# The first phase's norm factors move from the input to the sums, and the start of the kernel is put in another order

## The chip, the cores and the metric

The kernel runs on one core of a Trainium2 chip. The metric is the device time of one execution in microseconds (us); the kernel before takes 1038.08 us as the median of three runs (1037.84 to 1038.27). The engines are named as in the profile: PE (TensorE, matrix products), ACT (ScalarE), DVE (VectorE), POOL (GpSimd), and SP (SyncE, which here only issues DMAs).

## The reference

The reference is a trunk of two layers on x, 256 tokens of 1024 numbers in float32. Layer 0 is a SwiGLU feed-forward network (FFN), a hybrid mixer (state-space heads and attention heads), and a second FFN; layer 1 has a recurrent block in the middle. That makes six sub-layers, each of the form

```python
def rms_norm(x, g):
    y = xf * lax.rsqrt(jnp.mean(xf * xf, axis=-1, keepdims=True) + NORM_EPS)
    return y * g
def swiglu(x, w_in, w_out):
    gate, up = jnp.split(x @ w_in, 2, axis=-1)
    return (jax.nn.silu(gate) * up) @ w_out
...
h = swiglu(rms_norm(x, g[0]), ffn_w_in[layer, 0], ffn_w_out[layer, 0])
x = x + 0.5 * rms_norm(h, g[1])
```

The width inside an FFN is 2816, that is 22 blocks of 128 for the gate and 22 for the up part. The change concerns the first sub-layer alone: the first norm, and the product of its result with `ffn_w_in`.

The norm multiplies row i of x by one factor r_i = 1/sqrt(mean square + eps) and column k by g_k. Since the factor belongs to a whole row, (r x g) W = r (x g W): the factor can be applied to the input or to the sums.

## The kernel before, in words

The tokens are two tiles of 128 (t = 0, 1), the model width is eight blocks of 128 (k). Every product is made in split precision: a number is stored as a rounded high part and the remainder, and a product is the sum of high*high, high*low and low*high. Each weight slab (128 x 1024, 512 KB) is loaded by a DMA into one of five `raw` buffers, ScalarE writes the high part (`act.copy`, L271), and VectorE the remainder (L272). The function `prepare(n)` does this for the first n slabs of the program's order, and `load` issues the DMAs. The normed and transposed input, high and low, is the tile `xT`.

The instructions of PE stand in the order in which the code issues them (`tc.manual_schedule`). A plan lists the steps of each phase; generators, such as `hidden_of`, wait for a number of microseconds of a clock that the code keeps for itself (`LAG`) and are taken up between the steps by `catch_up`. The other engines are ordered by the framework's scheduler; the helper `behind`, and `turn` in the first norm, fix an order on one engine where it is wanted. On each engine the instructions run in order, so one that waits holds those behind it.

The FFN's plan for phase 0 begins with six A steps, A(f, t) for f = 0, 1, 2 and t = 0, 1. An A step makes the gate and up sums of 128 tokens for block f (`a_tile`): for each k one product 512 wide (input high with both weight parts) and one 256 wide (input low with weight high), added up in one PSUM tile, gate and up side by side. `mm_wide` puts the first wide product first, then the narrow ones, then the other wide ones; with `groups` it does so for a part of the k at a time. A block needs two slabs, one for k = 0 to 3 and one for k = 4 to 7. `hidden_of` adds the two halves of the sum (`halves`: ScalarE copies, VectorE adds), applies Silu on ScalarE (L542), multiplies with the up part on VectorE (L543), and later has PE transpose the result (L146), which is split again (L315). After these come 19 B steps, B(f), for f = 3 to 21, with the weights as the stationary side: the sums come out transposed, 128 hidden channels by 256 tokens, gate and up in two PSUM tiles, so that no transpose is needed. O steps multiply the hidden tiles with the output weights; the hidden tile of B(f) is used two B steps later. At the end of the phase three O groups of six products stand between B(21) and the first use of its hidden tile.

The first norm (`first_norms`) begins at the start of the program. Five products of a tile of ones (`WARM`) are put on PE while the first DMAs run. The norm's weight g comes as one row and is spread over all partitions by two products with a matrix whose first row is one (`gain`, two PSUM tiles). For each token tile ScalarE squares the two halves of x and adds up along the row (L431), GpSimd makes the factor (L322, L323, a power of -0.5), and VectorE multiplies x by the gain (L437, `xg`) and the identity by the factor (L417, `dg`). A product of a 128 x 128 block of `xg` with `dg` then transposes and scales in one (16 products, PSUM tiles `side`), and ScalarE and VectorE split the result into `xT` (L315). The splits of the first and second slab are placed between.

In all later phases `pre_norm` scales x before it is transposed; the change doesn't touch it.

## Time and profile before

| what | us |
|---|---|
| median of three runs (lowest, highest) | 1038.08 (1037.84, 1038.27) |
| the profiled execution | 1037.15 |
| its span, first instruction to last | 1035.4 |
| PE busy in the span | 1022.0 |
| DVE, ACT, POOL busy | 718.3, 598.8, 24.6 |
| first product of x with the first slab, in the chain | 11.93 |

The span is what the traces show; the profiled execution's own time lies 1.75 us above it. In the trace a product of two float32 tiles appears as two records, one in the split precision as one, and matmul records overlap a little: the chain of waits gives their lengths without the overlap. `raw` is a slab as loaded, `w` a split slab, `rot` and `side` are PSUM tiles, `hid` a split hidden tile, `h` a hidden tile before its transpose, `half` the copy of half a sum, `r` a norm factor. An instruction's length and the distance to the next one differ, as neighbours on one engine overlap.

### The profile page before, as it was taken

How to read it: one execution, taken by the hardware profiler on the slowest of the kernel's cores; microseconds unless marked ns; L12 is line 12 of the kernel's file. 1: busy time of each engine (PE TensorE's matmuls, PEld its weight loads, DVE VectorE, ACT ScalarE, POOL GpSimd, SP SyncE). 2: the span in 40 equal slices, each digit the busy share in tenths (PEclk: the TensorE clock that was granted, in tenths of full speed). 3: DMA queues.
4: the chain of work that ended last, by engine and by line, in shares of the span. 5: the costliest groups of instructions: out<-in, count | busy, mean ns of one | idle time of the engine just before them, and what ended most of it. 6: DMA issues, size and time to landing. Idle time of an engine off the chain costs nothing.

```text
span 1035.4 us, 16026 instructions
## 1 busy us (share of the span) xinstructions
PE 1022.0 (99%) x6084; PEld 898.7 (87%) x6084; DVE 718.3 (69%) x1158; ACT 598.8 (58%) x1062; POOL 24.6 (2%) x60
## 2 busy tenths in 40 slices
PE   8999999999999999999999999999999999999997
PEld 7888888999989988888888888888899978888886
DVE  7865557589898777755657685655769878555663
ACT  7655546466566566555556574544659867455551
POOL 1000000100000001000000100000010010000000
PEclk9999999999999999999999999999999999999999
DMA  8966556275745473855557285656735367655521
GB/s 289 329 212 193 196 182 214 77 230 176 222 153 170 140 264 105 296 185 185 185 183 225 81 299 190 191 187 191 234 114 184 107 219 272 211 182 190 183 82 41
DMA packets 55746, 195.91 MB, mean 189 GB/s; under 512 B 6972, under 2 KB 8148, under 8 KB 55668
## 3 DMA queue, kind: packets, MB, share of 16 engines
q1 hardware_dynamic: 52464, 190.04, 56.3%
q10 hardware_dynamic: 3204, 4.84, 1.4%
q8 instruction: 48, 0.79, 0.3%
q14 instruction: 30, 0.25, 0.1%
HBM read 193.78 MB, written 1.07 MB: 188 GB/s over the span
## 4 chain that ended last, share of the span: by engine, by line
PE 89%; DVE 4%; ACT 3%; issue 2%; DMA 1%; POOL 1%; DVEq 0%; POOLq 0%; ACTq 0%
PE rot L142 57%; PE side L142 31%; PE rot L146 1%; DVE c L606 1%; ACT junk L334 1%; ACT w L271 1%; DVE w L272 1%; DMA ca<-rows 0%; DMA raw<-in_rec_out_dram 0%; POOL r L323 0%; DVE sc L957 0%; DVE xn L350 0%; DVE x L388 0%; POOL r L322 0%; DVE sc L955 0%
## 5 line engine op out<-in xcount | busy, mean ns | idle before, releaser
L142 PE MATMUL rot<-xT,w 128*128 128x256 f32 (+1 forms) x3512 | 562.1, 318 | 0.0
L272 DVE TENSOR_TENSOR w<-raw,w 128x1024 fp32r<-128x1024 f32 (+1 forms) x349 | 423.8, 1219 | 190.2 <-ACT w L271 189.3
L142 PEld LDWEIGHTS rot<-xT,w 128*128 128x128 f32 x3512 | 494.6, 187 | 51.9 <-issue 1.3
L271 ACT CAST w<-raw 128x1024 fp32r<-128x1024 f32 (+1 forms) x349 | 366.1, 1053 | 164.1 <-DMA raw<-in_ffn_out_dram 139.0
L142 PE MATMUL side<-w,hid 128*128 128x512 f32 x1056 | 253.6, 390 | 0.0
L142 PEld LDWEIGHTS side<-w,hid 128*128 128x128 f32 x1056 | 197.4, 188 | 41.3
L142 PE MATMUL rot<-w,xT 128*128 128x256 f32 (+1 forms) x768 | 117.1, 310 | 0.3 <-DVE sg L288 0.2
L142 PEld LDWEIGHTS rot<-w,xT 128*128 128x128 f32 x768 | 103.5, 188 | 9.3 <-DVE sg L288 1.0
L315 ACT CAST hid<-up 128x256 fp32r<-128x256 f32 x76 | 31.0, 407 | 98.2 <-DVE up L573 98.1
L287 ACT COPY half<-rot 128x256 f32<-128x256 f32 x176 | 63.7, 363 | 16.9 <-PE rot L142 16.9
L315 DVE TENSOR_TENSOR hid<-up,hid 128x256 fp32r<-128x256 f32 x76 | 32.3, 425 | 30.1 <-ACT hid L315 30.1
L288 DVE TENSOR_TENSOR sg<-rot,half 128x256 f32<-128x256 f32 x100 | 41.9, 419 | 13.5 <-ACT half L287 13.2
L142 PE MATMUL side<-w,os 128*128 128x512 f32 x192 | 45.5, 393 | 0.0
L571 ACT ACTIVATE sg<-sg 128x256 f32<-128x256 f32 x76 | 31.8, 419 | 23.6 <-DVE sg L288 23.6
L142 PEld LDWEIGHTS side<-w,os 128*128 128x128 f32 x192 | 35.6, 188 | 7.2
L288 DVE TENSOR_TENSOR up<-rot,half 128x256 f32<-128x256 f32 x76 | 31.9, 419 | 3.1 <-ACT half L287 3.1
L573 DVE TENSOR_TENSOR up<-sg,up 128x256 f32<-128x256 f32 x76 | 31.9, 420 | 0.2
L385 DVE TENSOR_TENSOR xn<-side,g_post 128x512 f32<-128x512 f32 x24 | 16.4, 690 | 20.0 <-ACT junk L334 19.6
L322 POOL TENSOR_SCALAR r<-ms 128x1 f32<-128x1 f32 x24 | 7.3, 302 | 857.8 <-ACT junk L334 852.6
L334 ACT ACTIVATE junk<-side 128x512 bf16<-128x512 f32 x24 | 14.4, 598 | 22.9 <-PE side L142 22.0
L350 DVE SCALAR_TENSOR_TENSOR xn<-x,r,g_pre 128x512 f32<-128x512 f32 x20 | 14.1, 749 | 17.3 <-POOL r L323 17.3
L142 PE MATMUL side<-w 128*128 128x512 f32 x96 | 22.8, 393 | 0.9 <-DVE w L315 0.7
(195 smaller groups left out, 505.5 us busy)
## 6 DMA issues: line engine op xcount, KB each, us to landing
raw<-in_ffn_in_dram SPq DMA_DIRECT2D x176, 512.0 KB, 4.5
raw<-in_ffn_out_dram SPq DMA_DIRECT2D x88, 512.0 KB, 4.6
raw<-in_hyb_cols_dram SPq DMA_DIRECT2D x36, 512.0 KB, 4.4
raw<-in_hyb_out_dram SPq DMA_DIRECT2D x16, 512.0 KB, 3.6
raw<-in_hyb_v_dram SPq DMA_DIRECT2D x8, 512.0 KB, 4.6
raw<-in_rec_a_dram SPq DMA_DIRECT2D x8, 512.0 KB, 5.1
raw<-in_rec_cols_dram SPq DMA_DIRECT2D x8, 512.0 KB, 4.1
raw<-in_rec_out_dram SPq DMA_DIRECT2D x8, 512.0 KB, 3.5
```

The lines of the kernel that those rows point to most:

```text
L142: pe.matmul(ps, lhsT=lhsT, rhs=rhs, start=start, stop=stop)
L146: pe.transpose(ps, src, ident)
L271: splits[:] = [behind(act.copy(w[0][:, c], raw[:, c]), hold)]
L272: splits.append(behind(dve.tensor_tensor(w[1][:, c], raw[:, c], w[0][:, c].bitcast(F32), op=ALU.subtract), hold))
L287: act.copy(tmp, ps[:, 256:512])
L288: dve.tensor_tensor(dst, ps[:, 0:256], tmp, op=ALU.add)
L315: return act.copy(hi, src), dve.tensor_tensor(lo, src, hi.bitcast(F32), op=ALU.subtract)
L334: behind(act.activation(junk, src, func=AF.Square, scale=1.0 / (32.0 * weight), accum_out=ms[:, h:h + 1]), firsts)
L350: dve.scalar_tensor_tensor(xn[h], xt[:, cols], r, state["g_pre"][:, cols], op0=ALU.mult, op1=ALU.mult)
L385: behind(dve.tensor_tensor(hg[h], acc[h], state["g_post"][:, cols], op=ALU.mult), firsts)
L571: act.activation(sg, sg, func=AF.Silu)
L573: dve.tensor_tensor(up, sg, up, op=ALU.mult)
```

## The change

The factors of the first phase no longer go to the input. Instead of the 16 products with `dg`, plain transposes of `xg` (x times the gain) are made (`flips`), and the sums are multiplied by the factor: in `hidden_of` the Silu takes `rs[t]` as its scale and VectorE multiplies by `rs[t]` as well; in the B steps, where tokens lie along the row, a tile `factors` is made once by two products of the factor with the identity and a copy, and VectorE multiplies the gate sum and GpSimd the up sum by it.

The order at the start changes too. The row of g is loaded by ScalarE's queue, and SyncE's queue now holds x0, slab 0, x1, slab 1 and so on (before: the row, x0, x1, slab 0, slab 1). VectorE scales x0 by the gain; ScalarE copies the gain out of PSUM into `gains`, and GpSimd scales x1 with the copy. The first two slabs are split in two pieces each, in turn with x0's halves. A second set of five warm-up products follows x0's transposes. The first A step takes its k in four groups of two, and the transposes of x1 stand between these groups (`second`, a generator). Of the four squares one stays ahead of the first splits; the other three come behind the splits of x1.

```diff
-    sp.dma_start(g_row[0:32, :], norm_g[0, 0:1, :].broadcast_to([32, DM]))
+    act.dma_start(g_row[0:32, :], norm_g[0, 0:1, :].broadcast_to([32, DM]))
     xs = [res.tile([P, DM], F32, name=f"x{t}") for t in range(NT)]
-    for t in range(NT):
+
+    def x_load(t):
         sp.dma_start(xs[t], x_in[t * P:(t + 1) * P, :])
 
+    x_load(0)
...
-    def prepare(n):
+    def prepare(n, pieces=1):
...
-            splits[:] = [behind(act.copy(w[0][:, c], raw[:, c]), hold)]
-            splits.append(behind(dve.tensor_tensor(w[1][:, c], raw[:, c], w[0][:, c].bitcast(F32), op=ALU.subtract), hold))
+            splits[:] = []
+            for p in range(pieces):
+                c = slice(p * width // pieces, (p + 1) * width // pieces)
+                splits.append(behind(act.copy(w[0][:, c], raw[:, c]), hold))
+                splits.append(behind(dve.tensor_tensor(w[1][:, c], raw[:, c], w[0][:, c].bitcast(F32), op=ALU.subtract), hold))
             split[key] = w
             load(ready[0] + RAW)
...
+        def square(t, h):
+            junk = work.tile([P, 512], BF16, name="junk", bufs=1)
+            turn(act.activation(junk, xs[t][:, h * 512:(h + 1) * 512], func=AF.Square, scale=1.0 / 32.0,
+                                accum_out=ms[t][:, h:h + 1]))
+            if h:
+                turn(*rstd_of(rs[t], ms[t], 1.0))
+
+        def scaled(engine, t, h, g):
+            turn(engine.tensor_tensor(xg[t][:, h, :], xs[t][:, h * 512:(h + 1) * 512], g, op=ALU.mult))
+
+        def flips(t, h):
+            ps = side()
+            for k in range(4):
+                flip(ps[:, k * P:(k + 1) * P], xg[t][:, h, k * P:(k + 1) * P])
+            dst = [xT[:, 4 * h:4 * h + 4, j, t * P:(t + 1) * P] for j in range(2)]
+            return dst[0], dst[1], ps.rearrange("p (k c) -> p k c", k=4)
+
+        def weights(n, pieces=1):
+            hold[:] = latest.values()
+            prepare(n, pieces)
+            turn(*splits)
+
+        def second():
+            for h in range(2):
+                yield 0.9
+                held = flips(1, h)
+                turn(*split_to(*held))
+            square(0, 1)
+            weights(3)
+            square(1, 0)
+            square(1, 1)
+            hold[:] = latest.values()
+            normed.add((0, 1))
+            norms.discard((0, 1))
 
         warm = rot()
-        for _ in range(WARM):
-            mm(warm[:, 0:P], ones, ones, True, True)
-        gain, xg, dg, rs = [], [], [], []
-
-        def scale(t):
-            turn(dve.tensor_scalar(dg[t], ident, rs[t], None, op0=ALU.mult))
-
+
+        def busy(n):
+            for _ in range(n):
+                mm(warm[:, 0:P], ones, ones, True, True)
+
+        load(1)
+        x_load(1)
+        load(RAW)
+        busy(WARM)
+        gain = []
+        ms = [work.tile([P, 2], F32, name="ms", bufs=4) for _ in range(NT)]
+        rs.extend(work.tile([P, 1], F32, name="r", bufs=4) for _ in range(NT))
+        slot = wp.tile([P, 2 * SLAB + LINES], F32, name="w", bufs=SPLIT)
+        xg = [slot[:, t * DM:(t + 1) * DM].rearrange("p (h c) -> p h c", h=2) for t in range(NT)]
         for h in range(2):
             gain.append(rot())
             mm(gain[h], first, g_row[:, h * 512:(h + 1) * 512], True, True)
-        for t in range(NT):
-            ms = work.tile([P, 2], F32, name="ms", bufs=4)
-            r = work.tile([P, 1], F32, name="r", bufs=4)
-            rs.append(r)
-            xg.append(begin.tile([P, 2, 512], F32, name="xg", bufs=2))
-            dg.append(begin.tile([P, P], F32, name="dg", bufs=2))
-            for h in range(2):
-                src = xs[t][:, h * 512:(h + 1) * 512]
-                junk = work.tile([P, 512], BF16, name="junk", bufs=1)
-                turn(act.activation(junk, src, func=AF.Square, scale=1.0 / 32.0, accum_out=ms[:, h:h + 1]))
-                if h:
-                    for ins in rstd_of(r, ms, 1.0):
-                        turn(ins)
-                    if not t:
-                        scale(t)
-                turn(dve.tensor_tensor(xg[t][:, h, :], src, gain[h], op=ALU.mult))
-        scale(1)
+        square(0, 0)
+        gains = begin.tile([P, NT, 512], F32, name="gains")
+        for h in range(2):
+            scaled(dve, 0, h, gain[h])
+            turn(act.copy(gains[:, h, :], gain[h]))
+        held = [flips(0, h) for h in range(2)]
+        busy(WARM)
+        for h in range(2):
+            scaled(pool, 1, h, gains[:, h, :])
+
         hold[:] = latest.values()
-        prepare(1)
-        for ins in splits:
-            turn(ins)
-        for t in range(NT):
-            for h in range(2):
-                ps = side()
-                for k in range(4):
-                    c = slice(k * P, (k + 1) * P)
-                    mm(ps[:, c], xg[t][:, h, c], dg[t], True, True)
-                dst = [xT[:, 4 * h:4 * h + 4, j, t * P:(t + 1) * P] for j in range(2)]
-                for ins in split_to(dst[0], dst[1], ps.rearrange("p (k c) -> p k c", k=4)):
-                    turn(ins)
-                if h and not t:
-                    hold[:] = latest.values()
-                    prepare(2)
-                    for ins in splits:
-                        turn(ins)
-            normed.add((0, t))
-        hold[:] = latest.values()
+        prepare(1, 2)
+        one = list(splits)
+        turn(*one[0:2])
+        turn(*split_to(*held[0]))
+        turn(*one[2:4])
+        turn(*split_to(*held[1]))
+        weights(2, 2)
+        normed.add((0, 0))
+        norms.add((0, 1))
         start_pool.__exit__(None, None, None)
-
+        spawn(second())
+
+    rs = []
     xT = new_xT(0)
     first_norms(xT)
...
+        def factors():
+
+            if not laid:
+                laid.append(hid.tile([P, NT * P], F32, name="factors"))
+                ps = rot()
+                for t in range(NT):
+                    mm(ps[:, t * P:(t + 1) * P], rs[t].broadcast_to([P, P]), ident, True, True)
+                act.copy(laid[0], ps[:, 0:256])
+            return laid[0]
...
-                act.activation(h32[:, 0:P], sg[:, 0:P], func=AF.Silu)
-                dve.tensor_tensor(h32[:, P:256], h32[:, 0:P], sg[:, P:256], op=ALU.mult)
+                if ph:
+                    act.activation(h32[:, 0:P], sg[:, 0:P], func=AF.Silu)
+                    dve.tensor_tensor(h32[:, P:256], h32[:, 0:P], sg[:, P:256], op=ALU.mult)
+                else:
+                    act.activation(h32[:, 0:P], sg[:, 0:P], func=AF.Silu, scale=rs[t])
+                    dve.scalar_tensor_tensor(h32[:, P:256], sg[:, P:256], rs[t], h32[:, 0:P], op0=ALU.mult, op1=ALU.mult)
...
                 until(lambda: (ph, t) in normed)
-                ps = a_tile(xT, t, s, (KT,) if ph or f else (KT // 2, KT // 2))
+                ps = a_tile(xT, t, s, (KT,) if ph or f or t else (2, 2, 2, 2))
                 until(lambda: len(turning) < 2)
...
                 halves(sg, pg)
+                if not ph:
+                    dve.tensor_tensor(sg, sg, factors(), op=ALU.mult)
                 act.activation(sg, sg, func=AF.Silu)
                 halves(up, pu)
+                if not ph:
+                    pool.tensor_tensor(up, up, factors(), op=ALU.mult)
                 dve.tensor_tensor(up, sg, up, op=ALU.mult)
...
         def gains():
             if not ph:
-                yield 10.0
+                yield 12.0
             state["g_post"] = g_tile(l, j + 1, "g_post")
```

On PE the start of the stream moves. `rot<-ones` are warm-up products, `rot<-g_row,first` the gains, `side<-dg,xg` the products that transpose and scale, `side<-ident,w` the plain transposes (the tile `xg` now lies in a slab buffer `w`), and `rot<-w,xT` the A steps. Before:

```order
L142 MATMUL rot<-ones 128x128 x5
L142 MATMUL rot<-g_row,first 128x512 x2
L142 MATMUL side<-dg,xg 128x128 x16
L142 MATMUL rot<-w,xT 128x512
L142 MATMUL rot<-w,xT 128x256 x4
L142 MATMUL rot<-w,xT 128x512 x3
L142 MATMUL rot<-w,xT 128x256 x4
```

Now, from the transposes of x0 on:

```order
L146 MATMUL side<-ident,w 128x128 x8
L142 MATMUL rot<-ones 128x128 x5
L142 MATMUL rot<-w,xT 128x512
L142 MATMUL rot<-w,xT 128x256 x2
L142 MATMUL rot<-w,xT 128x512
L142 MATMUL rot<-w,xT 128x256 x2
L142 MATMUL rot<-w,xT 128x512 x2
L146 MATMUL side<-ident,w 128x128 x4
L142 MATMUL rot<-w,xT 128x256 x2
L142 MATMUL rot<-w,xT 128x512 x2
L146 MATMUL side<-ident,w 128x128 x4
L142 MATMUL rot<-w,xT 128x256 x2
```

The 16 products in front of the first A step are gone; eight transposes and five warm-up products stand there, and two sets of four transposes stand inside the first A step.

On ScalarE the rows from the second slab on to the fourth and fifth: `raw` gives the slab (before: `raw_145` is slab 1, `raw_147` slab 2, `raw_149` slab 3; now `raw_107`, `raw_109`, `raw_111`), `half<-rot` are the copies of A(0,0)'s and A(0,1)'s sums. Before:

```order
L271 CAST w_169<-raw_145 128x1024
L315 CAST xT_103<-side_174 128x4x128
L315 CAST xT_103<-side_181 128x4x128
L271 CAST w_192<-raw_147 128x1024
L271 CAST w_197<-raw_149 128x1024
L271 CAST w_202<-raw_151 128x1024
```

Now:

```order
L276 CAST w_164<-raw_107 128x512 x2
L320 CAST xT_102<-side_184 128x4x128
L320 CAST xT_102<-side_195 128x4x128
L418 ACTIVATE junk_202,ms_120<-x0_83 128x512
L292 COPY half_222<-rot_175 128x256
L276 CAST w_206<-raw_109 128x1024
L588 ACTIVATE h32_225<-sg_221,r_122 128x128
L418 ACTIVATE junk_211,ms_121<-x1_84 128x512
L418 ACTIVATE junk_213,ms_121<-x1_84 128x512
L292 COPY half_271<-rot_253 128x256
L276 CAST w_228<-raw_111 128x1024
L588 ACTIVATE h32_274<-sg_270,r_123 128x128
```

Slabs 2 and 3 followed directly on the second tokens' `xT`; now a square, a copy of a sum and, ahead of slab 3, a Silu, two more squares and the copy of A(0,1)'s sums stand before them.

On PE behind B(3) (`rot<-xT,w` is a B step, `side<-w,hid` an O step), before:

```order
L142 MATMUL rot<-xT,w 128x512 x2
L142 MATMUL rot<-xT,w 128x256 x16
L142 MATMUL rot<-xT,w 128x512 x14
L142 MATMUL side<-w,hid 128x512 x6
L146 MATMUL rot<-ident,h_379 128x128
L142 MATMUL side<-w,hid 128x512 x12
L146 MATMUL rot<-ident,h_407 128x128
```

Now:

```order
L142 MATMUL rot<-xT,w 128x512 x2
L142 MATMUL rot<-xT,w 128x256 x16
L142 MATMUL rot<-xT,w 128x512 x14
L142 MATMUL rot<-ident,r 128x128 x2
L146 MATMUL rot<-ident,h_386 128x128
L142 MATMUL side<-w,hid 128x512 x12
L146 MATMUL rot<-ident,h_414 128x128
L142 MATMUL side<-w,hid 128x512 x12
```

The two products `rot<-ident,r` are added, and the transposes of two hidden tiles move by one O group. From there on the rows of all engines are the same but for the added multiplications in the B steps of phase 0: 19 rows on VectorE, L618, one in each B step, and 19 on GpSimd, L622.

## Rows read from the trace of the kernel before

**Rows 1.** The page's first part: engine, busy us, share, instructions.
```profile
PE 1022.0 (99%) x6084; PEld 898.7 (87%) x6084; DVE 718.3 (69%) x1158; ACT 598.8 (58%) x1062; POOL 24.6 (2%) x60
```

**Rows 2.** Chain of waits over the start: start us, us, what.
```profile
7.88 4.04 PE side L142 x32
11.93 8.37 PE rot L142 x48
20.30 0.11 PE rot L146
...
29.15 5.53 PE rot L142 x32
```

**Rows 3.** Timeline of TensorE, first 13 us: start, length, instructions.
```profile
1.10 2.50 PE L142 MATMUL rot<-ones 128*128 128x128 f32 x10 [1.10 <-DVE ones L188]
3.48 2.38 PE L142 MATMUL rot<-g_row,first 128*128 128x512 f32 x4
```

**Rows 4.** Timeline of VectorE at the start, shapes kept apart.
```profile
5.05 0.69 DVE L437 TENSOR_TENSOR xg<-x,rot 128x512 f32<-128x512 f32 x1 [2.44 <-PE rot L142]
...
13.20 1.28 DVE L315 TENSOR_TENSOR xT<-side,xT 128x512 fp32r<-128x512 f32 x2
14.40 2.35 DVE L272 TENSOR_TENSOR w<-raw,w 128x1024 fp32r<-128x1024 f32 x2
```

**Rows 5.** Timeline of the SyncE queue at the start.
```profile
1.24 0.89 SPq L185 DMA_DIRECT2D x<-in_x_dram  x2
2.16 13.81 SPq L252 DMA_DIRECT2D raw<-in_ffn_in_dram  x8
```

**Rows 6.** DMAs issued at 1.24 and 2.16: KB, us to landing.
```profile
x<-in_x_dram SPq DMA_DIRECT2D x1, 512.0 KB, 3.7
...
raw<-in_ffn_in_dram SPq DMA_DIRECT2D x1, 512.0 KB, 5.8
```

**Rows 7.** Timeline of ScalarE at the start, shapes kept apart.
```profile
4.98 0.63 ACT L431 ACTIVATE junk<-x 128x512 bf16<-128x512 f32 x1 [2.70 <-DMA x<-in_x_dram]
...
5.73 0.63 ACT L431 ACTIVATE junk<-x 128x512 bf16<-128x512 f32 x1
6.27 0.19 ACT L431 ACTIVATION_READ_ACCUMULATOR junk<-x 128x1 f32 x1
...
11.40 1.15 ACT L315 CAST xT<-side 128x512 fp32r<-128x512 f32 x2
12.45 2.95 ACT L271 CAST w<-raw 128x1024 fp32r<-128x1024 f32 x3
15.30 0.37 ACT L287 COPY half<-rot 128x256 f32<-128x256 f32 x1
15.56 1.06 ACT L271 CAST w<-raw 128x1024 fp32r<-128x1024 f32 x1
...
18.64 0.30 ACT L542 ACTIVATE h<-sg 128x128 f32<-128x128 f32 x1
```

**Rows 8.** The page's costliest groups: the post-norm's VectorE line.
```profile
L385 DVE TENSOR_TENSOR xn<-side,g_post 128x512 f32<-128x512 f32 x24 | 16.4, 690 | 20.0 <-ACT junk L334 19.6
```

**Rows 9.** Windows of TensorE: us, busy (count), granted clock, DMA.
```profile
7.88:11.93 4.05, 4.05 (x33) 1.00 1.00 406
```

**Rows 10.** Timeline of GpSimd at the start.
```profile
2.07 0.29 POOL masks.py:199 TENSOR_SCALAR_AFFINE_SELECT ident<-ident 128x128 f32<-128x128 f32 x1
...
6.94 0.57 POOL L323 TENSOR_TENSOR r<-r,power 128x1 f32<-128x1 f32 x1
```

**Rows 11.** Timeline of VectorE, last B tile of phase 0.
```profile
179.60 0.42 DVE L288 TENSOR_TENSOR sg<-rot,half 128x256 f32<-128x256 f32 x1 [1.47 <-ACT half L287]
...
183.40 0.43 DVE L315 TENSOR_TENSOR hid<-up,hid 128x256 fp32r<-128x256 f32 x1 [0.47 <-ACT hid L315]
```

**Rows 12.** Chain of waits at the end of phase 0.
```profile
180.69 12.24 PE side L142 x54
```

**Rows 13.** GpSimd's groups by line: busy, mean ns, idle before.
```profile
L323 POOL TENSOR_TENSOR r<-r,power 128x1 f32<-128x1 f32 x24 | 13.5, 563 | 2.0
```

14 lines of the change are left out of this document (7 added, 7 removed).

## The prediction

> **What bounds the kernel now.** I read the page's first part, then the chain of waits over the start, then each engine's timeline there. TensorE is busy for 99% of the span [rows 1], so a change gains only where it lets TensorE's stream of weight products begin earlier, or takes instructions out of it. In the chain that stream begins at 11.93 us: 48 products of three tiles A(f, t) run 8.37 us without a gap, and further tiles follow after single transposes [rows 2]. One A tile is 16 products, eight 512 wide and eight 256 wide, and takes 2.79 us (8.37 / 3): 0.233 for a wide one, 0.116 for a narrow one. So A(0,0) ends at 14.72, A(0,1) at 17.51, A(1,0) at 20.30. In front of the stream stand 16 products of the row-scaled input, 4.04 us from 7.88, and these waited for the norm factor. That is what the change attacks. I compare the moment when A(1,0) ends, because everything after it hangs on TensorE alone.
>
> **The start, worked out anew.** All times are from the span's start; a spacing is the distance between the starts of two neighbours.
>
> Until 5.86 nothing can move: five warm-up products end at 3.60, the two gain products at 5.86 [rows 3], and VectorE's first scaling starts at 5.05 when the first gain is there [rows 4]. x and the first slab arrive in time: x0 was issued at 1.24 and took 3.7 us (4.94), slab 0 as third came at 2.16 + 5.8 = 7.96 [rows 5, 6]; that is 1.5 us per transfer, so in the new order slab 0 comes by 6.5, x1 by 8.0, slab 1 by 9.5. The norm row moves to another queue; 128 KB in front of x become 128 KB beside x, which I cost at nothing, as it is needed at 3.48 only. If it came 0.5 us late, all below would come 0.5 later.
>
> VectorE scales x0's halves 5.05 to 5.74 and 5.88 to 6.57 (0.69 each [rows 4]). ScalarE squares the first half (0.75 spacing [rows 7]) and copies both gains out of PSUM; two engines that read one PSUM tile do so in turn here, as VectorE's post-norm does behind ScalarE's square of the same sums [rows 8]. So the copies start at 5.77 and 6.60. If they need not wait, the second starts 0.35 earlier. From 7.13 ScalarE rounds slab half, x half, slab half, x half, with 0.5 us for a slab half (half of 0.98, from three casts in 2.95) and 0.525 for an x half (two in 1.05) [rows 7]: the starts are 7.13, 7.65, 8.15, 8.7, then slab 1's halves from 9.5.
>
> VectorE follows with the remainders, 0.6 us each (two x halves in 1.28, a whole slab 1.14 [rows 4]), and is the slower: starts 7.75, 8.3, 8.9, 9.5, 10.1, 10.7. TensorE makes its first four transposes at 5.9 and the next at 6.6 (0.11 each [rows 2]), and then five warm products, 1.25 us at the rate of the 16 products (0.25 each): it is free at 8.4. [...] The first A product goes at 8.45, the narrow ones at 9.0, when the first x remainder is there. From 9.0 I find no wait: the rest of the tile is 2.79 - 0.23 = 2.56 and the eight transposes of the second tokens inside it are 0.88. A(0,0) ends at about 12.5 and A(0,1) at 15.3, each 2.2 us earlier than now.
>
> **What takes most of it back.** ScalarE's queue now holds more work ahead of the third and fourth slabs. The last x half of the second tokens can be rounded when its transposes are done, 0.70 us (the last group) before A(0,0) ends, at 11.85. Behind it stand, in ScalarE's order: the square of x0's second half, the copy of A(0,0)'s sums, slab 2, the Silu of A(0,0), two squares of x1, the copy of A(0,1)'s sums, and only then slab 3. With the spacings 0.53, 0.75, 0.26, 0.95, 0.2 (a Silu takes 0.30, and neighbours overlap by about 0.1), 0.75, 0.75 and 0.26 [rows 7] slab 3 starts at 16.3 and is rounded at 17.35; nothing in this row of work waits (the Silu needs the norm factor, done 13.1 + 1.05 = 14.15, from the end of the read of the accumulator at 6.46 to the end of the power at 7.51 [rows 7, 10]; the copy of A(0,1) needs 15.3). VectorE adds 1.22: slab 3's remainder is there at 18.6. In the kernel now these two slabs are split before 16.75 [rows 4], with TensorE needing them at 17.5. In the changed kernel TensorE comes to A(1,0) at 15.3, waits 0.4 for slab 2's remainder, about 1.0 for slab 3's rounding, and again some 0.1 for its remainder; its last four wide products, 0.93, end at 19.55. So at the end of A(1,0) the gain is 20.30 - 19.55 = 0.75 us.
>
> **The rest of the phase.** The tiles that follow find their slabs split (slabs 4 and 5 at 20 and 21.2, needed at 22.5), so the 0.75 is carried on. Two products of the factors against the identity come into the stream behind B3's products [rows 2]: 2 x 0.25 = 0.5 us, with nothing beside them. The first phase's 19 B tiles get one more VectorE multiplication each (0.42, the length of the sum's addition) and one of GpSimd. VectorE idles 1.47 us in front of such an addition at the end of the phase [rows 11] and a hidden tile is used two B tiles later, so this is hidden. The narrowest place is the last B tile: its remainder is done at 183.83 [rows 11], and TensorE needs the hidden tile first at 180.69 + 3 x 1.36 = 184.77 (54 products in 12.24 [rows 12]). VectorE's multiplication stands before a slab split that waits for ScalarE, so it costs nothing; GpSimd's stands in the chain. For 256 columns of two operands the trace has no row. The nearest: 0.29 us for 128 columns of one operand, of which some 0.1 is fixed, and 0.56 for one column of a power [rows 10, 13]. That makes 0.5 for one operand, and 0.9 for two read in turn; bounds 0.3 (VectorE does it in 0.42) and 1.5. I take 0.9: the chain ends at 184.7, TensorE does not wait. At 1.5 it would lose 0.4 us.
>
> **GpSimd in the start.** By the same rows a multiplication of 512 columns is 0.9 for one operand and 1.7 for two; bounds 0.5 and 3. From 8.0 two of them end at 11.4 with 1.7 each, when TensorE comes for the second at 11.35. I take 1.5. [...]
>
> **Sum.** -0.75 + 0.5 = -0.25 us. The profiled execution took 1037.15 us (span 1035.4 and 1.75 around it), which makes 1036.9; the median of the runs shown is 0.93 higher, so 1037.8.
>
> **The rivals.**
> 1. *The gain is kept.* If slab 3 isn't late (ScalarE gets through its row faster, or the squares are cheaper beside others), the 2.2 us stay: -2.2 + 0.5 = -1.7, 1036.4. For it: A(0,0) itself is bounded by few steps. Against it: the eight ScalarE instructions are in one order, and each has a row.
> 2. *GpSimd holds TensorE inside A(0,0).* TensorE takes its instructions in order, so the second tokens' transposes stop the stream until GpSimd is done. With p us for one multiplication the loss over my sum is 8.0 + 2p - 11.35; it begins at p = 1.7, the kernel is slower than before from p = 1.8, and by over 2 us from p = 2.85. At p = 2.5: +1.4, 1039.5. For it: no row of this size, and VectorE busy beside it. Against it: one operand of 128 columns takes 0.29.
> 3. *GpSimd's first multiplication is slow to begin.* Before, the first of the 24 powers took 0.57 us, as their mean of 0.563 [rows 10, 13], with no gap in front beyond the usual; a first use costs nothing there. [...] Worked out from the rows: if the first multiplication began d us late, the two would end at 11 + d, and the kernel would lose d - 0.6 against before (11 + d - 11.35 - 0.25); it is slower by over 2.1 us from d = 2.7, and d = 4 gives 1041.5.
> 4. *The clock falls before the second warm-up.* The first five products took 2.50 us, twice the later rate [rows 3]; then TensorE would be free at 9.65 and the narrow products would go at 9.9 and not at 9.0: 0.9 - 0.25 = +0.65, 1038.7. Against it: the clock granted after the idle time [rows 9].
>
> **Chances.** My forecast 0.58, rival 1 0.17, rival 2 0.13, rival 3 0.03, rival 4 0.05, something unseen 0.04. A measurement of this kernel tells about 0.2%, 2.1 us, from no change; only rival 1 with a little more, or something unseen, reaches faster (0.09), and rivals 2 and 3 at their upper ends reach slower (0.10). The likeliest case alone spans 1037.0 to 1038.8 (ScalarE's steps 0.3 either way, the norm row 0.5 late, the last B tile 0.4). The range reaches to rival 1 below and to rival 2 with p = 2.6 above: 1036.2 to 1039.8.
>
> **What would show it.** Right: the first A product near 8.5; A(0,1)'s sums near 15.3; then TensorE waiting for slab 3 for 1 us or more; A(1,0)'s end near 19.6; 0.5 us of `rot<-ident,r` behind B3; GpSimd's wide multiplications under 1.7 us. Wrong: a wait of the transposes for GpSimd; A(1,0) without a wait; a wait at the last B tile of the phase; any new wait behind 200 us.

## The result and the profile after

The changed kernel takes 1043.57 us (median of five runs, 1042.51 to 1044.55); the kernel before took 1037.92 beside it (1037.19 to 1038.27). The ratio is 1.0053, with a 95% interval of 1.0042 to 1.0065: slower by 5.65 us, where the forecast was 1037.8 and at most 1039.8. The profiled execution took 1043.57 with a span of 1041.8, 6.4 us over the span of before.

The page of the changed kernel: its first part, and the chain that ended last by engine; the last line is that chain in the kernel before. TensorE's share in the chain is the first thing to see: 63% where it was 89%, with VectorE, DMA and ScalarE in it for the rest. Busy time alone [rows 1] says almost nothing of the change.

```profile
PE 1025.3 (98%) x6082; PEld 898.9 (86%) x6082; DVE 732.2 (70%) x1175; ACT 600.8 (58%) x1067; POOL 44.1 (4%) x81
...
PE 63%; DVE 12%; DMA 11%; ACT 7%; issue 4%; POOL 1%; DVEq 0%; POOLq 0%; ACTq 0%; SPq 0%
```

```profile
PE 89%; DVE 4%; ACT 3%; issue 2%; DMA 1%; POOL 1%; DVEq 0%; POOLq 0%; ACTq 0%
```

**The start.** TensorE's timeline (start, length, instructions, idle time in front and what ended it). The gain products, which began at 3.48 [rows 3], begin at 5.10, after 1.49 us of waiting for the norm row; and they take 3.75 us, not 2.38. The first A product comes at 12.25, and the tile A(1,0) waits 0.64 us for a slab's rounding. The last line is the pair of factor products.

```profile
5.10 3.75 PE L142 MATMUL rot<-g_row,first 128*128 128x512 f32 x4 [1.49 <-DMA g_row<-in_norm_g_dram]
...
10.12 1.28 PE L142 MATMUL rot<-ones 128*128 128x128 f32 x10
12.25 1.94 PE L142 MATMUL rot<-w,xT 128*128 128x512 f32 x8 [0.85 <-ACT xT L320]
...
21.15 2.46 PE L142 MATMUL rot<-w,xT 128*128 128x256 f32 x11 [0.64 <-ACT w L276]
23.45 0.28 PE L146 MATMUL rot<-ident,h 128*128 128x128 f32 x1
...
37.83 0.60 PE L142 MATMUL rot<-ident,r 128*128 128x128 f32 x4
```

As a mark for the whole start I use the transpose that comes right behind A(1,0). In the timeline of before it stands at 20.14 (20.30 in the chain, without the overlap [rows 2]):

```profile
20.14 0.27 PE L146 MATMUL rot<-ident,h 128*128 128x128 f32 x1
```

So TensorE is 3.3 us late at this point. ScalarE's timeline of the changed kernel, with what stands in front of the fourth slab (the cast at 20.05): both copies of the gain wait for VectorE, and three squares lie ahead of that slab.

```profile
7.91 0.59 ACT L473 COPY gains<-rot 128x512 f32<-128x512 f32 x1 [1.66 <-DVE w L424]
9.61 0.59 ACT L473 COPY gains<-rot 128x512 f32<-128x512 f32 x1 [1.12 <-DVE w L424]
...
16.29 0.63 ACT L418 ACTIVATE junk<-x 128x512 bf16<-128x512 f32 x1
...
18.42 0.62 ACT L418 ACTIVATE junk<-x 128x512 bf16<-128x512 f32 x1
...
19.17 0.63 ACT L418 ACTIVATE junk<-x 128x512 bf16<-128x512 f32 x1
...
20.05 1.05 ACT L276 CAST w<-raw 128x1024 fp32r<-128x1024 f32 x1
```

**The end of phase 0.** Here the chain of before was TensorE alone [rows 12]. In the changed kernel the same stretch of the chain runs through VectorE, ScalarE and GpSimd, and the last B step's hidden tile comes 0.71 us too late for TensorE, at 189.24 (the chain, then TensorE's timeline):

```profile
184.94 0.96 ACT w L276
...
185.92 1.23 DVE w L277
...
187.56 0.74 POOL up L622
188.33 0.43 DVE up L623
188.78 0.41 ACT hid L320
...
189.24 2.79 PE side L142 x11
```

```profile
189.24 3.02 PE L142 MATMUL side<-w,hid 128*128 128x512 f32 x12 [0.71 <-ACT hid L320]
```

**Behind it** there is one more wait of the kind, in a later phase none of whose instructions were changed; before has none there.

```profile
737.43 4.83 PE L142 MATMUL rot<-xT,w 128*128 128x512 f32 x27 [0.78 <-DVE sg L293]
```

I laid TensorE's products of the two traces side by side, counted from the last. The lateness of the changed kernel is 3.31 us behind A(1,0), 3.77 behind the factor products, 4.64 behind the last B step of phase 0, 5.7 behind 737 us and 5.80 at the end. The remaining 0.6 of the 6.4 us of span is behind TensorE's last product (last section).

### The profile page after: what moved, and what is told of

It reads as the page before. It is cut to its first block, busy times and chain, and to the rows that moved or that the text cites. A ratio compares the mean times of both kernels' runs of the same rounds, so it can differ in the third digit from the quotient of the medians.

```text
span 1041.8 us, 16075 instructions
## 1 busy us (share of the span) xinstructions
PE 1025.3 (98%) x6082; PEld 898.9 (86%) x6082; DVE 732.2 (70%) x1175; ACT 600.8 (58%) x1067; POOL 44.1 (4%) x81
## 4 chain that ended last, share of the span: by engine, by line
PE 63%; DVE 12%; DMA 11%; ACT 7%; issue 4%; POOL 1%; DVEq 0%; POOLq 0%; ACTq 0%; SPq 0%
PE rot L142 40%; PE side L142 22%; DMA raw<-in_ffn_out_dram 11%; DVE w L277 6%; ACT w L276 4%; DVE sg L293 1%; ACT junk L339 1%; PE rot L146 1%; DVE c L656 1%; DVE xn L355 0%; DMA raw<-in_rec_out_dram 0%; POOL r L328 0%; DVE up L293 0%; DVE x L393 0%; DVE sc L1007 0%
## 5 line engine op out<-in xcount | busy, mean ns | idle before, releaser
L277 DVE TENSOR_TENSOR w<-raw,w 128x1024 fp32r<-128x1024 f32 (+1 forms) x351 | 431.2, 1234 | 182.0 <-ACT w L276 180.7
```

Of the source, the lines that this page charges most:

```text
L277: splits.append(behind(dve.tensor_tensor(w[1][:, c], raw[:, c], w[0][:, c].bitcast(F32), op=ALU.subtract), hold))
```

## The experiments

Each kernel ran beside the kernel before on the same chip. The third column is the difference of the two medians, and the ratio is to the kernel before. The chips differ: the medians of before lie between 1036.94 and 1037.92, so where two of the runs below are compared, the difference of their third columns stands in brackets. The marks are of one execution each; in ten traces with the change's own start (the change and runs 4, 6, 7, 9, 10 and 13 to 16) they lie between 22.90 and 23.56.

| run | us | above before | ratio (95%) | mark behind A(1,0) |
|---|---|---|---|---|
| the change | 1043.57 | 5.65 | 1.0053 (1.0042, 1.0065) | 23.45 |
| 1 norm row on SyncE's queue | 1041.58 | 4.02 | 1.0039 (1.0025, 1.0053) | 21.43 |
| 2 eight warm-up products | 1043.26 | 5.70 | 1.0057 (1.0045, 1.0070) | 22.61 |
| 3 before, row on ScalarE's queue | 1038.60 | 1.04 | 1.0007 (0.9998, 1.0016) | 21.28 |
| 4 no factors in the B steps | 1040.66 | 3.10 | 1.0030 (1.0018, 1.0041) | 22.90 |
| 5 fourth slab ahead of the squares | 1042.49 | 5.51 | 1.0057 (1.0042, 1.0073) | 22.42 |
| 6 up multiplied on VectorE | 1043.07 | 6.09 | 1.0058 (1.0045, 1.0070) | 23.35 |
| 7 no multiplication of up | 1043.33 | 6.35 | 1.0052 (1.0040, 1.0065) | 23.56 |
| 8 start alone (1, 4 and 5) | 1037.79 | 0.81 | 1.0005 (0.9997, 1.0014) | 20.29 |
| 9 no multiplication of the gate | 1041.39 | 4.18 | 1.0039 (1.0025, 1.0053) | 23.08 |
| 10 factor products only | 1041.36 | 4.15 | 1.0038 (1.0026, 1.0051) | 23.02 |
| 11 x1 scaled by VectorE | 1043.33 | 6.12 | 1.0060 (1.0046, 1.0074) | 22.32 |
| 12 mended, complete | 1039.32 | 2.11 | 1.0020 (1.0011, 1.0028) | 20.26 |
| 13 gate multiplied in the first ten B steps | 1043.40 | 6.46 | 1.0061 (1.0048, 1.0074) | 23.31 |
| 14 gate multiplied in the last nine | 1042.18 | 5.24 | 1.0052 (1.0038, 1.0066) | 23.50 |
| 15 the change, one more execution | 1044.31 | 7.37 | one time | 23.34 |
| 16 as 7, one more execution | 1041.49 | 4.55 | one time | 23.11 |

### 1. The norm row back on SyncE's queue

```diff
-    act.dma_start(g_row[0:32, :], norm_g[0, 0:1, :].broadcast_to([32, DM]))
+    sp.dma_start(g_row[0:32, :], norm_g[0, 0:1, :].broadcast_to([32, DM]))
```

> One line of the change undone: the row of g is loaded by SyncE's queue again, ahead of x0; all else as in the changed kernel. Theory (the row comes late on ScalarE's queue): TensorE does not wait for the row, the second gain is done near 5.9 us and not at 8.85, the first A product goes near 9.3 and not at 12.25, A(1,0) ends near 20.6 and not at 23.6, and the time falls by 3 us, to 1040.5. Rival (ScalarE's row of squares and GpSimd beside VectorE make most of the loss): the time falls by under 1 us, to 1042.6 or more, although the gains come early.

TensorE's timeline in that run: the gain products no longer wait, but still take a microsecond more than before.

```profile
3.55 3.38 PE L142 MATMUL rot<-g_row,first 128*128 128x512 f32 x4
```

The mark moves from 23.45 to 21.43 and the median falls by 2.0 us (1.6), where I had expected 3. The queue is the largest single part of the start's loss. The wait is not the only reason for slow gain products: here there is none, and they still take 3.38 us.

### 2. Eight warm-up products in front of the gain products

```diff
-        busy(WARM)
+        busy(WARM + 3)
         gain = []
```

> The changed kernel with eight warm-up products ahead of the gains in place of five, so that TensorE is not idle until the row lands at 5.1 us. Theory (the gain products are slow because TensorE was idle before them): the two gain products take about 2.0 us after 5.1 and not 3.75, and the time falls by 1.5 to 2 us, to 1041.7. Rival (they are slow whatever stands before them; only the landing counts): the pair still takes 3.7 us, and the time stays within 0.3 us of 1043.6.

The wait for the row is filled (the products end at 4.89), and the gain products take 2.53 us, near the 2.38 of before. The mark improves by 0.84 to 22.61, and the time stays: this profiled execution (1045.71, the slowest of its five) shows, at 167 us, a wait of 2.5 us for VectorE's `sg` that the change's first trace does not have. So an earlier mark need not show in the time: what TensorE gains at the start can be lost at the end of the phase.

### 3. The kernel before with the row on ScalarE's queue

The one line of the change, put into before.

> The kernel before, with the row of g loaded by ScalarE's queue, and nothing else changed. Theory: the row lands at about 5.1 us here too, the second gain is done near 8.9, and VectorE's scalings of x, which stand ahead of the first slab's remainder, end 1.1 us later; the time rises by 1.0 to 1.3 us, to 1039.1. Rival (the row is late only because x0 and slab 0 go in turn with it in the new order): the row lands by 3.5 us and the time stays at 1038.

```profile
4.80 3.75 PE L142 MATMUL rot<-g_row,first 128*128 128x512 f32 x4 [1.19 <-DMA g_row<-in_norm_g_dram]
```

Wait and slow gain products appear in before as well, and the mark is 1.14 us later; the median rises by 1.04 us, which the interval of the ratio does not tell from nothing. So the queue's price at the start doesn't need the rest of the change; in the changed kernel the mark loses more by it (2.0), which I put down to the new start hanging on the gain products as a whole, without a run that tests this.

### 4. No factors in the B steps

Left out: both multiplications of the 19 B steps, the factor products and their copy.

```diff
-                if not ph:
-                    dve.tensor_tensor(sg, sg, factors(), op=ALU.mult)
...
-                if not ph:
-                    pool.tensor_tensor(up, up, factors(), op=ALU.mult)
```

> The changed kernel without the factors on the gate and up sums of the 19 B steps (the two products, the copy, and the 19 multiplications each of VectorE and GpSimd are left out, so the B steps' sums are not scaled). Theory (the products cost 0.45 us in the stream, and GpSimd's multiplication in the last B step makes TensorE wait 0.9 us): the time falls by 1.3 us, to 1042.3, and A(1,0) ends at 23.6 as before. Rival (GpSimd beside VectorE's remainders delays slabs in the whole phase and what follows it): the time falls by 2.5 us or more.

2.9 us less than the change (2.6): the rival. There is no wait at the end of the phase, and the lateness of TensorE stays at 2.8 us from the mark to the end. So about half of the loss lies in the B steps, where I had put 0.5.

### 5. The fourth slab split ahead of the squares

```diff
-            weights(3)
+            weights(4)
             square(1, 0)
```

> The changed kernel with slab 3 split ahead of the two squares of x1 on ScalarE. Theory (the prediction's: ScalarE's row holds A(1,0)): TensorE's wait of 0.6 us for slab 3's rounding in A(1,0) goes, A(1,0) ends 0.6 to 1.0 us earlier against A(0,1)'s end, and the time falls by as much, to 1042.8. Rival (the wait moves to slab 2's remainder or to the Silu of A(0,1), or the gain is lost again later in the phase): the time stays within 0.3 us of 1043.6.

```profile
15.50 7.09 PE L142 MATMUL rot<-w,xT 128*128 128x256 f32 x36
22.42 0.27 PE L146 MATMUL rot<-ident,h 128*128 128x128 f32 x1
```

The wait for the slab is gone (36 products in one piece, where the change has 25 and then 11 behind a wait), and the mark is 1.0 us earlier. In the median this doesn't show: the executions lie between 1039.88 and 1044.71. The other kernels derived from the change that multiply the gate in B steps scatter by 1.4 to 3.9 us; those that don't multiply it (runs 4, 9, 10) by 0.7 to 1.0. This is a hint and no more, as five times are few: run 8 doesn't multiply it either, and its eleven times scatter by 2.2. The profiled execution, the fastest of the four, has no wait at the end of phase 0 although it does all the multiplications.

### 6. The multiplication of up on VectorE

```diff
-                    pool.tensor_tensor(up, up, factors(), op=ALU.mult)
+                    dve.tensor_tensor(up, up, factors(), op=ALU.mult)
```

> The changed kernel with the up sums of the B steps multiplied by the factors on VectorE in place of GpSimd. Theory (GpSimd's multiplication runs beside VectorE's slab remainder and stretches it from 1.23 to 1.7 us, which delays the slabs step by step until TensorE waits near the phase's end): no remainder of the phase is longer than 1.25 us, the last slabs come 1.5 to 3 us earlier, TensorE does not wait at the last B step, and the time falls by 1.5 to 2.5 us, to 1041.5, although VectorE does 19 multiplications more. Rival (VectorE's added work is what delays the slabs): the time rises, to 1044 or more.

No gain, and TensorE still waits, 0.85 us, at the last B step; so GpSimd's place in the chain isn't the cause. Two lines say why the two are about equal: the groups of VectorE's slab remainders by form, in the change and then here.

```profile
L277 DVE TENSOR_TENSOR w<-raw,w 128x1024 fp32r<-128x1024 f32 x346 | 427.5, 1241 | 180.8 <-ACT w L276 179.6
```

```profile
L277 DVE TENSOR_TENSOR w<-raw,w 128x1024 fp32r<-128x1024 f32 x346 | 420.6, 1220 | 181.1 <-ACT w L276 180.0
L622 DVE TENSOR_TENSOR up<-up,factors 128x256 f32<-128x256 f32 x19 | 8.0, 419 | 0.1
```

Given to GpSimd, the 19 multiplications lengthen VectorE's remainders by 6.9 us in all (run 7, without them, has 420.2); done by VectorE they take 8.0. The offload saves VectorE hardly anything.

### 7. No multiplication of up

Left out: GpSimd's multiplication in the B steps; VectorE's stays.

> The changed kernel without GpSimd's multiplication of the up sums (they are left unscaled); the factor products and VectorE's multiplications stay. Theory: as with the multiplication on VectorE, the remainders take 1.23 us; the time falls by 2.0 to 2.5 us, to 1041.3, and the run without any factors (1040.7) is better only by the two products, 0.45 us, and little more. Rival (the delay comes from VectorE's multiplication of the gate sums, which stands in front of the slab remainders): it falls by under 0.8 us.

No gain in the median, where I had expected 2.0 to 2.5 us, but here it is a poor guide: the five times are 1041.73, 1041.74, 1043.33, 1043.35 and 1043.48. In the profiled one TensorE doesn't wait at the end of phase 0, and waits 1.06 us for VectorE's `sg` at 1000.79, in a phase with no changed instruction (run 16 takes this up).

### 8. The new start alone

Runs 1, 4 and 5 together: the B steps' factors are left out, the row is on SyncE's queue, the fourth slab comes first.

> The changed kernel with three things at once: the row of g on SyncE's queue, slab 3 split ahead of the squares of x1, and no factors on the B steps' sums (these stay unscaled). It shows what the new order of the start gives by itself. Theory (the three losses add up: 2.0 + 0.7 + 2.9): 1038.0, no better than the kernel before at 1037.6, because VectorE's remainder beside GpSimd's multiplication takes 0.7 us more at the start. Rival (the start as the prediction worked it out gains 2.2 us once nothing else is in the way): 1036.

```profile
3.70 2.71 PE L142 MATMUL rot<-g_row,first 128*128 128x512 f32 x4
...
9.15 2.33 PE L142 MATMUL rot<-w,xT 128*128 128x512 f32 x8 [0.18 <-DVE w L277]
...
12.44 0.73 PE L142 MATMUL rot<-w,xT 128*128 128x512 f32 x2 [0.29 <-DVE w L277]
```

The time is that of before within the interval: the three parts account for the loss. It also shows what the new start is worth without them: nothing. The first A product comes 2.5 us earlier (9.15 for 11.68 in the timeline of before), A(0,1) starts 0.4 earlier (14.15 for 14.54), and the mark isn't earlier at all. Of the 2.7 us that TensorE takes longer between 9.15 and the mark, the eight transposes inside A(0,0) are 0.7. The rest is in products that start 0.1 to 0.45 us later than their neighbours' rate would have them, most of them where VectorE's remainder of a slab half or of an `xT` half comes late; only one of these shows as idle time in the lines above (0.29 us).

### 9. No multiplication of the gate

Left out: VectorE's multiplication in the B steps; GpSimd's stays.

```diff
-                    dve.tensor_tensor(sg, sg, factors(), op=ALU.mult)
```

> The changed kernel without VectorE's multiplication of the gate by the factors in the first phase's B steps (the gate stays unscaled, so this part of the computation is left out); GpSimd's multiplication, the factor products and their copy stay. Theory: VectorE's added work in the B steps, ahead of Silu and so of ScalarE's later work, is what makes TensorE wait at the end of the first phase and later; then the time falls by about 2 us below the changed kernel, to 1041.0 to 1041.6, with no wait at the last B step. Rival: VectorE's multiplication lies beside other work like GpSimd's, and the two-stage chain as a whole, whichever engine does it, or the products and the copy are the price; then the time stays within 0.8 us of the changed kernel, 1042.8 to 1043.6.

2.2 us less than the change (1.5; the intervals of the two ratios overlap), and none of the waits: without VectorE's multiplication of the gate, GpSimd's costs nothing (1041.39 here, and run 10, which has neither, takes 1041.36). Windows of the end of phase 0 (PE, PEld, DVE, ACT, POOL busy with counts, clock, DMA share, GB/s), for before, the change, and this run:

```profile
150.00:185.00 35.00, 35.00 (x186) 30.16 (x185) 24.61 (x37) 19.82 (x35) 0.00 (x0) 1.00 0.65 213
```

```profile
150.00:185.00 35.00, 35.00 (x195) 30.44 (x194) 28.20 (x39) 20.32 (x36) 3.81 (x5) 1.00 0.58 192
```

```profile
150.00:185.00 35.00, 35.00 (x194) 30.48 (x193) 24.43 (x36) 19.60 (x36) 6.53 (x5) 1.00 0.65 198
```

VectorE goes from 24.6 to 28.2 of 35 us, and back to 24.4 without its multiplication. The work has shifted by some 4 us against before, so the windows hold about the same pieces and not exactly the same.

### 10. Factor products without the multiplications

Left out: both multiplications; the products and the copy stay.

> The changed kernel with the two factor products and the copy of them, but without both multiplications of the first phase's B steps (gate and up stay unscaled there, so this part of the computation is left out). Theory: the products cost 0.45 us of TensorE's stream and nothing else, the multiplications the rest; then the time is the one without all factors, 1040.66, and 0.45 more: 1041.1, with a narrow spread, no wait at the last B step, and a shift of TensorE's stream that is constant behind 38 us. Rival: the tile of the factors, the PSUM buffer that they take or the copy cost what was missing; then it is 1042.5 to 1043.6.

As expected within 0.3 us. VectorE's timeline at the last B step of that run, beside the same place of the change: here VectorE has caught up, and idles 1.60 us until TensorE's sums are there, as in before [rows 11]; in the change it comes straight from other work.

```profile
182.90 0.42 DVE L293 TENSOR_TENSOR sg<-rot,half 128x256 f32<-128x256 f32 x1 [1.60 <-ACT half L292]
```

```profile
185.04 0.42 DVE L293 TENSOR_TENSOR sg<-rot,half 128x256 f32<-128x256 f32 x1
```

### 11. The second tokens scaled by VectorE

```diff
-        gains = begin.tile([P, NT, 512], F32, name="gains")
...
-            turn(act.copy(gains[:, h, :], gain[h]))
...
-            scaled(pool, 1, h, gains[:, h, :])
+            scaled(dve, 1, h, gain[h])
```

> The changed kernel with the second tokens scaled by VectorE out of PSUM, as the first are, without ScalarE's two copies of the gains and without GpSimd. Theory: GpSimd costs at the start what it saves: VectorE's piece beside it took 1.36 us in place of 0.68, and ScalarE's copies stood in front of the first slab's rounding; two multiplications of 0.69 on VectorE in their place leave the end of tile A(1,0) within 0.5 us of 23.6, and the time within 0.6 us of the changed kernel. Rival: GpSimd's share and the copies are a main part of the start's loss; then A(1,0) ends at 22.5 or before, and the time falls by 1 us or more.

Run 10 began its gain products at the same moment (4.80 and 4.82), so the marks can be compared: 23.02 with GpSimd and the copies, 22.32 without. By these two traces they cost 0.70 us rather than saving time: between my two expectations, but nearer the rival. The median doesn't show it. This profiled execution, the slowest of its four, waited 1.6 us at 165.8 and 1.5 at the last B step.

### 12. A complete, mended version

Runs 1, 5 and 6 together; nothing is left out.

> A complete version: the changed kernel with the norm row back on SyncE's queue, the fourth slab split ahead of the squares, and the multiplication of up on VectorE. Theory: the start then equals that of before (as in the run of the start alone, 1037.8), the factor products add 0.45 us, and VectorE's multiplications 0 to 3 us at the end of the first phase: 1038.3 to 1041, not below the kernel before. Rival: the losses don't add, and the start's gain is kept: 1037.4 or less.

Of all complete versions of the new kernel this is the fastest, 4.3 us below the change (3.5), and 2.1 above before. Its start is level with before (20.26), the factor products add 0.45, and two waits of TensorE at the end of phase 0 make up most of the rest:

```profile
PE side L142 <- ACT hid L320: 1.0, 1, 1.0
PE rot L142 <- DVE sg L293: 0.5, 1, 0.5
```

No run points to a version below both kernels, since the start alone gains nothing that could pay for the factors.

### 13 and 14. The multiplication of the gate in a part of the B steps

Left out: VectorE's multiplication in the last nine B steps (13), or in the first ten (14).

```diff
-                if not ph:
+                if not ph and f < 13:
                     dve.tensor_tensor(sg, sg, factors(), op=ALU.mult)
```

> The changed kernel with VectorE's multiplication of the gate in the first ten B steps of the first phase only; in the last nine the gate stays unscaled, so that part of the computation is left out. Theory: the multiplication costs time where VectorE has least to spare, at the end of the phase; then this kernel is near the one without any of them, 1041.2 to 1041.9, without a wait at the last B step. Rival: each step's multiplication adds its share, or the cost doesn't lie in the steps at all; then it is half way or above, 1042.3 to 1043.6.

> The changed kernel with VectorE's multiplication of the gate in the last nine B steps of the first phase only; in the first ten the gate stays unscaled, so that part of the computation is left out. Theory: the last steps cost the time; then this kernel is as slow as the changed one, 1042.8 to 1043.8, with a wait for the hidden tile at the last B step. Rival: each step adds its share: 1042.0 to 1042.6.

My theory had the last steps as the dear ones, and the traces speak against it. With the multiplication in the first ten steps alone TensorE waits at the end of phase 0, in steps that have none of it:

```profile
165.69 5.96 PE L142 MATMUL rot<-xT,w 128*128 128x512 f32 x32 [0.67 <-DVE sg L293]
...
190.84 4.40 PE L142 MATMUL side<-w,hid 128*128 128x512 f32 x18 [1.34 <-ACT hid L320]
```

With it in the last nine alone, phase 0 has no wait. The medians (1043.40 and 1042.18) point the same way, though their intervals overlap. The two traces are no even pair: that of 13 is one of the two slowest of its five executions (1044.81 of 1041.54 to 1045.03), that of 14 one of the two fastest (1041.92 of 1041.63 to 1043.62). So they show that late waits can come without the late multiplications, and not what each part of the steps costs. What links the early steps with the late waits is the row of slabs. The table gives how much later than in before VectorE begins a slab's remainder, for some of the last slabs of the stretch up to 186 us, counted from its end (in us; in brackets the time in before):

| slab | change | change again (15) | no gate (9) | first ten (13) | last nine (14) |
|---|---|---|---|---|---|
| 36th (88.55) | 3.05 | 4.08 | 3.07 | 4.46 | 3.22 |
| 25th (116.61) | 4.43 | 7.12 | 3.07 | 5.62 | 2.78 |
| 16th (143.04) | 2.91 | 5.35 | 0.95 | 4.99 | 1.78 |
| 8th (162.85) | 4.69 | 6.73 | 2.54 | 6.71 | 3.72 |
| 2nd (175.67) | 6.46 | 8.49 | 3.71 | 7.87 | 5.48 |
| TensorE before its waits | 3.77 | 3.66 | 3.80 | 3.63 | 3.80 |
| added at the end of phase 0 | 0.9 | 3.0 | 0 | 2.6 | 0 |

The slabs' lateness falls by 0.6 to 2.1 us from the 25th to the 16th slab and grows by 2.8 to 3.7 from there to the 2nd. TensorE waits where it has grown to 6 us or more while TensorE itself is 3.7 late. Taken over all traces, what counts is the 2nd slab's lateness less TensorE's own. It is -0.1 us in the five without the gate's multiplication (runs 3, 4, 8, 9, 10), and 1.0 to 6.9 in the twelve with it. TensorE waits at the last B step in the eight of these with 2.7 or more (the change 2.7, run 15 4.8, run 12 4.6), and in none of the four with 2.2 or less (runs 5, 7, 14, 16). So the gate's multiplication makes the last slabs late in every trace, but whether that reaches TensorE differs from execution to execution. One piece of the change's chain shows how it is handed on: the load of a slab begins at 156.19, just where a remainder ends and frees its buffer, and takes 4.58 us; two loads before it stand in the chain in the same way (from 137.17 and 145.41). A late remainder makes a late load, and that a late remainder.

### 15 and 16. One more execution of two kernels

> The changed kernel itself, one more execution looked at. Theory: the wait at the end of the first phase (0.7 us in the first trace) belongs to the kernel and is there again within 0.3 us; the wait in a later phase belongs to single executions and is elsewhere or gone. Rival: both are at the same places, so both belong to the kernel.

> The changed kernel without GpSimd's multiplication of up (that part of the computation is left out), one more execution looked at. Theory: no wait at the end of the first phase, as in the first trace, and the wait of 1.06 us in the last phase is elsewhere or gone. Rival: the wait in the last phase stands where it was.

TensorE's waits for VectorE and ScalarE in the B steps of the change's second execution:

```profile
PE side L142 <- ACT hid L320: 1.5, 1, 1.5
...
PE rot L142 <- DVE sg L293: 0.5, 1, 0.5
```

The wait at the end of phase 0 belongs to the kernel, but not its size: 0.9 us of lateness in one execution, 3.0 in the other (I had expected 0.3 of difference). The wait at 737 us is gone, and so is the one at 1000.79 in run 16, which took 1041.49 with no wait for `sg` or `hid`. So those later waits come in single executions. Without GpSimd's multiplication three of six times lie near 1041.6, the level without the gate's multiplication, and three near 1043.4.

## Why the prediction was wrong

The forecast was a gain of 0.75 us at the end of A(1,0), 0.5 lost to the factor products, and nothing behind them. In the change's trace TensorE is 3.31 us late at that mark, loses 0.46 to the factor products, 0.9 at the end of phase 0 and 1.1 in later phases, and the program ends 0.6 later behind the last product. Three steps failed: the norm row's queue at no cost, the stream of A(0,0) without a wait, and the multiplications of the B steps as hidden.

**The norm row** ("which I cost at nothing ... If it came 0.5 us late, all below would come 0.5 later"). The dependence was right, the size wrong: the row held TensorE back by 1.49 us, and with it back on SyncE's queue the mark is 2.0 earlier (run 1). The gain products also ran at half the rate for longer (a record every 0.85 us and not 0.43, last section), 3.75 us and not 2.38, for which I had no term: I had taken them at their length from before [rows 3], as if it belonged to the instruction. The idle time in front is at most a part of that: with it they take 3.44 to 3.75 us in all traces, without it 2.38 to 3.38 (3.38 in run 1, 3.27 in run 12). The same move makes the program end 0.6 us later (last section); I had no term for that either.

**The second warm-up** ran in 1.28 us (1.25 forecast). Rival 4 didn't come about.

**"From 9.0 I find no wait."** Wrong, and not only through the late start. In run 8 the first A product comes at 9.15, 0.7 behind my 8.45 (its gain products end 0.57 behind my 5.86). A(0,1) starts 0.4 us earlier than in before and not 2.2, and by the end of A(1,0) nothing is left. A(0,0) takes 5.0 us there, where 2.86 in before and 0.7 for the transposes make 3.6. I followed the slab halves up to 10.7 and took the rest as supplied, with 0.6 for each remainder; beside GpSimd they take up to 1.2 there and 1.36 in the change. So the forecast of a gain of 2.2 us at A(0,0) has no counterpart in any run, and rival 1, which kept it, falls too.

**"What takes most of it back"**: the mechanism was right. Three squares stand ahead of the fourth slab, and TensorE waits 0.64 us for its rounding; with the slab moved ahead the mark is 1.0 earlier (run 5), where I had about 1.0 and 0.1.

**Factor products**: 0.5 forecast, 0.46 measured.

**"VectorE idles 1.47 us in front of such an addition ... so this is hidden."** This is the step that failed worst: I put nothing, and the gate's multiplication costs 2.2 us (1.5 against the kernels before of their own chips). The row [rows 11] is right, but it stands at the one place where VectorE has already caught up. In the steps ahead of it VectorE waits for ScalarE and ScalarE for VectorE in turn (in before, in the step from 172.92, VectorE 0.47 us twice and ScalarE 1.63 once), and there is less to spare. The timeline of before shows the same instruction in two B steps in a row:

```profile
172.92 0.43 DVE L315 TENSOR_TENSOR hid<-up,hid 128x256 fp32r<-128x256 f32 x1 [0.47 <-ACT hid L315]
...
177.70 0.43 DVE L315 TENSOR_TENSOR hid<-up,hid 128x256 fp32r<-128x256 f32 x1 [0.47 <-ACT hid L315]
```

and in the changed kernel:

```profile
179.21 0.42 DVE L320 TENSOR_TENSOR hid<-up,hid 128x256 fp32r<-128x256 f32 x1 [0.47 <-ACT hid L320]
...
184.70 0.43 DVE L320 TENSOR_TENSOR hid<-up,hid 128x256 fp32r<-128x256 f32 x1 [0.48 <-ACT hid L320]
```

TensorE takes 6.89 us for a B step with an O group (5.53 + 1.36). VectorE needed 4.78 per step and caught up 2.1 each; now it needs 5.49 and catches up 1.4. The longer period comes with the multiplication of up: it is 5.50 in run 9, with GpSimd's alone, and 4.95 in run 7, with the gate's alone. It doesn't decide by itself: in run 9 VectorE comes to these steps 2.6 us earlier than in the change and is done in time, and in run 7 there is no wait either. By these traces it takes both, lateness carried in from the steps before, which comes with the gate's multiplication, and less room to make it good. The times of run 7 show it less clearly, as three of six are as long as the change's. One hidden multiplication is a bad model all the same: 19 of them stand in a row of loads and splits that hands on what it is late. The two prices: 2.2 us (1.5) for the gate's multiplication with GpSimd's beside it (run 9), and 0.7 (1.05) for the products by run 10 against run 4, 0.46 in the trace. My sum for the last B step had a slip besides: with 1.5 us for GpSimd it gives a wait of 0.56 us, not 0.4. How much comes from which step, and why the slabs of one and the same kernel are 2.7 us later in one execution than in another (25th slab of the table), I did not settle.

**GpSimd** in the start took 1.27 us for 512 columns (1.5 forecast, 1.7 the limit) and never held TensorE: rival 2 falls. In run 8, where VectorE's remainders came first, the two took 1.82 and 1.73, and TensorE's transposes did not wait for them there either. Rival 3 falls too: the first multiplication began 0.07 us after its operand was there (8.50, 8.57). The 256 columns took 0.73 to 0.86 (0.9 forecast) where VectorE's remainder had not begun first. What I had not counted is the other side: VectorE's instruction beside it is often the one that gets longer. VectorE's and GpSimd's timelines, first at the start, then in two B steps:

```profile
10.75 1.36 DVE L277 TENSOR_TENSOR w<-raw,w 128x512 fp32r<-128x512 f32 x1 [1.17 <-ACT w L276]
...
12.63 0.68 DVE L277 TENSOR_TENSOR w<-raw,w 128x512 fp32r<-128x512 f32 x1
...
51.66 1.23 DVE L277 TENSOR_TENSOR w<-raw,w 128x1024 fp32r<-128x1024 f32 x1
...
145.95 1.67 DVE L277 TENSOR_TENSOR w<-raw,w 128x1024 fp32r<-128x1024 f32 x1 [0.23 <-ACT w L276]
```

```profile
10.28 1.28 POOL L424 TENSOR_TENSOR w<-x,gains 128x512 f32<-128x512 f32 x1 [0.43 <-ACT gains L473]
...
51.77 1.72 POOL L622 TENSOR_TENSOR up<-up,factors 128x256 f32<-128x256 f32 x1 [10.32 <-DVE up L293]
...
145.80 0.74 POOL L622 TENSOR_TENSOR up<-up,factors 128x256 f32<-128x256 f32 x1 [7.51 <-DVE up L293]
```

Half a slab takes 1.36 beside GpSimd and 0.68 alone; at 145.95 GpSimd is still busy until 146.54, and VectorE's remainder ends about as late as if it had begun then (1.67 for 1.23). At 51.77 VectorE's remainder had begun 0.11 us before, and it was GpSimd that took long (1.72 for 0.74). In each of these three places the later of the two ends within 0.15 us of where it would have ended had it begun when the earlier was done. It is not so for every instruction of VectorE: its scaling of x0's second half, which reads the gain out of PSUM, began at 8.89 beside GpSimd's first multiplication (8.57 to 9.84) and took 0.69 us, as the first half did alone. No run was made to find what decides it.

**"Any new wait behind 200 us"** was named as a sign of error. There was one at 737.43, but not in every execution (it is gone in run 15, as run 7's is in run 16); why a phase of unchanged instructions waits in some executions stays open, as does why the gain products' rate rises at another moment in each run.

## What to carry to other kernels

Idle time in front of one instruction is no slack if it is read where the engine has just caught up (here 1.47 us before the last addition to the gate sum, and the gate's multiplication cost 2.2): take the engine's period over several steps, compare it with the consumer's, and look whether what one step is late is handed on by loads that wait for a buffer (here the load at 156.19). The 19 multiplications given to GpSimd beside VectorE's slab remainders cost VectorE almost as much as doing them itself (6.9 us for 8.0), so look at the length of what runs beside before counting such a move as a saving. And before crediting an earlier start, follow every supplier up to the point where the time is compared; an advance of 2.5 us at the first product, 0.7 of it transposes that had only been moved behind it, was worth nothing 11 us later.
